# Forgetting attention in a two-layer decoder trunk: the causal mask added by VectorE, the softmax division moved to the reload of the outputs, the gate's weights in one operand

## The chip, the cores and the metric

The kernel runs on one core of a Trainium2 chip. The metric is the device time of one execution in microseconds; the time given for a kernel is the median of its runs. The core has a matrix engine (TensorE, in the profile PE, with its weight loads as PEld), a vector engine (VectorE, DVE), an engine for activation functions (ScalarE, ACT), a general engine (GpSimd, POOL) and an engine that here issues all transfers (SyncE, SP). Matrix products are accumulated in PSUM, a memory of eight banks of 128 partitions by 512 float32 numbers; everything else lies in SBUF or in DRAM.

## What is computed

A trunk of two layers on a sequence of 1024 positions with 1024 features, all in float32. Layer 0 mixes by a gated convolution, layer 1 by forgetting attention with 16 heads of 64 features; after the mixer each layer has a cross-attention into 256 memory tokens and a squared-ReLU MLP of 4096 inner features. Every sublayer is preceded by an RMS norm and added to the residual stream. The change touches the attention of layer 1:

```python
hk = rmsnorm(x, kv_norm_g)
kvf = hk @ kvf_w                       # keys, values and 16 gate columns
log_f = log_sigmoid(kvf[..., 2 * D:] + fgate_b)
c = cumsum(log_f, axis=1)              # one running sum per head
...
s = q @ k.T / sqrt(64) + (c[query] - c[key])
s = where(key_pos <= query_pos, s, -inf)
p = softmax(s)
out = (p @ v) @ w_o
```

Since `c[query]` is the same for a whole row of the softmax, it falls out; only `c[key]` has to be subtracted.

## The kernel before

The activations lie transposed: features on the partitions, in eight chunks of 128, positions along the free dimension, in two halves of 512. To keep float32 accuracy on a faster matrix format, an operand is split into a high part (a copy rounded by ScalarE) and a low part (the difference, by VectorE): `split`, lines 150 to 152. A product of two split operands is three passes (`passes`, line 262): low × high, high × low, high × high.

**The order of the work.** The program is written in the order in which the author wants it; a scheduler orders each engine's instructions ahead of the run, from that order and from its own estimate of times. Inside `in_order` blocks the order of the text is kept for the engines named. Tiles come from pools: tiles with the same `tag` share a fixed number of buffers (`bufs`), and a later tile takes a buffer that an earlier one has left. The pool `nrm` has a tag "t" with four buffers of 128 x 512, which normalization, sums of squares, loads of stored tensors and many other steps share.

**Layer 1, `fox_layer` (line 1111).** The MLP of layer 0 ends by normalizing the first half of the positions and loading the first two weight pieces (`start_fox`). `fox_layer` then prepares the gate weights `wf` as two tiles, high and low (lines 1123 to 1128), runs the first half of the first key and query products and of the gate product (24 passes, line 1136), normalizes the second half, and calls `attend`.

**`attend` (line 1155)** builds the causal mask (0 on and below the diagonal, -1e30 above), copies it and the identity matrix to the matrix format (`maskr`, `identr`), and runs two generators beside each other until the first pair of heads has keys and queries: `projections` (line 1230), which yields after every three passes, and `forget_gates` (line 1195), which forms the sigmoid's logarithm and the running sum `c` and writes it to DRAM (`cd`). Then come the 16 heads, each with eight blocks of 128 queries. For each head the row `c` is loaded back into all 128 partitions (`cj`). For each block:

- `attention_scores` (line 1294): two passes per 512 keys into one of two PSUM banks (pool `p2`), and on the last, diagonal column block a third product, identity × mask (line 1308); VectorE subtracts `cj` and takes the row maximum in one instruction (line 1310), negates it (1313); ScalarE takes the exponential and the row sum `rs` (1315); VectorE forms the reciprocal (1316) and multiplies the probabilities by it (1321; for odd blocks of the last two heads ScalarE does it, 1319).
- three blocks later (`DELAYS`), `attention_transposes` (line 1324): the probabilities are transposed by TensorE in float32 into banks of the pool `pm` (four banks) and split.
- for every second block, one step after that, `attention_output` (line 1347): 256 queries of output for one head, whose two value parts are added up by ScalarE and VectorE (`ol`), and written to DRAM (`od`, line 1359).
- three steps of the projections for the next pair of heads, as work for TensorE in between.

**The end.** Lines 1143 to 1148 load the outputs back from `od`, 16 tiles `o` of 128 x 512 (chunk by chunk, first half and second half of the positions), and split them into the operand tiles `hs`, whose buffers are free once the last projection has read the previous ones. The residual stream is loaded back from `xd` (16 transfers, line 134), and line 1153 multiplies by `fox_wo`: all eight output chunks for the first half of the positions, then all eight for the second. An output needs all eight chunks of its operand.

Of the kernel before, what the change touches and what calls it, by code (L numbers as in the profile page):

```python
# [12 lines left out]
F32 = mybir.dt.float32  # L13
F32R = mybir.dt.float32r
AF = mybir.ActivationFunctionType
ALU = mybir.AluOpType
# [70 lines left out]
def trunk(ctx, tc, a, out):  # L87
# [1023 lines left out]
    def fox_layer(xd, hs, ws, seconds):  # L1111
        nonlocal X, xpool
        cd = dram.tile([HEADS, S], F32, name="cd")
        od = dram.tile([NCH, P, S], F32, name="od")

        early = {}
        with (
            banks(4) as pm,
            tc.tile_pool(name="fs", bufs=2, space=PSUM, reuse_waits="tile") as p2,
        ):  # L1120

            with in_order({mybir.EngineType.PE, mybir.EngineType.DVE, mybir.EngineType.Activation}):
                wf = [nrm.tile([P, NCH, HEADS], F32R, name=f"wf{x}", bufs=1) for x in "hl"]
                raw = nrm.tile([P, NCH, HEADS], F32, name="wf", tag="t", bufs=4)
                nc.sync.dma_start(raw, a["wf"])
                g = par[:, COLS["kv"] : COLS["kv"] + NCH].unsqueeze(2).to_broadcast([P, NCH, HEADS])
                dve.tensor_tensor(raw, raw, g, op=ALU.mult)
                split(*wf, raw)
# [6 lines left out]
                early["gate"] = bank(pm)[:HEADS, :]  # L1135
                product(early["gate"], by_weights(wf, hs, HALVES[0]))
                normalize(hs, None, HALVES[1], rb)
                ws.append(weights(a["wv"][0], gain="kv"))
            xpool.close()
            xpool = ExitStack()  # L1140
            with tc.tile_pool(name="fa", bufs=2) as bp:
                attend(bp, p2, pm, ws, wf, hs, early, cd, od)
        hs = operands()
        for m in range(NCH):
            for sl in HALVES:
                o = nrm.tile([P, HALF], F32, name="o", tag="t", bufs=4)
                nc.sync.dma_start(o, od[m, :, sl])
# [7 lines left out]
    def attend(bp, p2, pm, ws, wf, hs, early, cd, od):  # L1155
# [12 lines left out]
        late = []  # L1168

# [11 lines left out]
        for head in range(HEADS):  # L1181
            cj = bp.tile([P, S], F32, name="cj")
            nc.sync.dma_start(cj, cd[head : head + 1, :].to_broadcast([P, S]))
            for b in range(8):
                while head not in tiles:
                    next(project)
                x = attention_scores(bp, p2, tiles[head], head, b, cj, identr, maskr)
                late.append((DELAYS[0], partial(attention_transposes, bp, pm, tiles[head], head, b, x, od)))
                late = run(late)
                for _ in range(3):  # L1190
                    next(project, None)
        while late:
            late = run(late)

    def forget_gates(bp, wf, hs, cd, early):

        fb = bp.tile([HEADS, 1], F32, name="fb", bufs=1)
# [3 lines left out]
        for sl in HALVES:  # L1201
            if sl.start == 0:
                t = early["gate"]
            else:
                t = bank(ps)[:HEADS, :]
                product(t, by_weights(wf, hs, sl))
            dve.tensor_scalar(z[:, sl], t, fb[:, 0:1], None, op0=ALU.add)
# [86 lines left out]
    def attention_scores(bp, p2, tiles, head, b, cj, identr, maskr):  # L1294
# [5 lines left out]
        mx = -3e38  # L1300
        for j in range(0, n, HALF):
# [4 lines left out]
            pe.matmul(s, qb, kh[:, sl], start=False, stop=not last)  # L1306
            if last:
                pe.matmul(s[:, b * P - j :], identr, maskr, start=False, stop=True)
# [4 lines left out]
        dve.tensor_scalar(nb, mx, -1.0, None, op0=ALU.mult)  # L1313
        rs = bp.tile([P, 1], F32, name="rs")
        act.activation(x[:, :n], x[:, :n], AF.Exp, bias=nb, accum_out=rs)  # L1315
        dve.reciprocal(rs, rs)
        if head >= HEADS - 2 and b % 2:

            act.activation(x[:, :n], x[:, :n], AF.Copy, scale=rs)
        else:  # L1320
            dve.tensor_scalar(x[:, :n], x[:, :n], rs, None, op0=ALU.mult)
# [124 lines left out]
```

## Time and profile before

| | us |
|---|---|
| median of three runs | 2823.84 |
| the three runs | 2826.63, 2823.84, 2814.29 |
| the profiled execution | 2825.31 |
| its span, first to last instruction | 2823.3 |
| TensorE busy | 2740.8 (97% of the span) |
| VectorE busy | 2030.9 (72%) |
| ScalarE busy | 1278.3 (45%) |
| start of attention to the end of its output projection, about | 1349 to 1976 |

The page of the profile gives the share of each engine over the whole span; since the stages differ, the views used below cut it by time. A row of the table by stretches begins with the bounds of the stretch in microseconds from the span's start and its length; then come the busy microseconds of PE, PEld, DVE, ACT and POOL with the number of instructions in brackets, the granted clock of TensorE (1.00 is full), the busy share of the transfer engines and what they moved in GB/s. A row of a group of instructions has the line, the engine, the operation, what is written and read, the count, the busy time, the mean in nanoseconds, and the idle time just before them with what ended it. A row in order of time has the start, the length, the engine and the line; `xN` says that N like instructions were merged. For transfers the last number is the median time from issue to landing.

### The profile page before, as it was taken

What the parts mean: (1) busy time and instruction counts of PE and PEld (TensorE: products, weight loads), DVE (VectorE), ACT (ScalarE), POOL (GpSimd) and SP (SyncE); (2) the same over time, 40 slices, a digit from 0 to 9 for tenths busy, and PEclk for the clock granted to TensorE, in tenths of its full rate; (3) what the DMA queues carried; (4) which work ended last, traced back from release to release, by engine and by line L of the source; (5) the groups of instructions that cost most, each with busy time, mean ns of one, the idle gap of its engine ahead of it and who ended that gap; (6) DMA issues with size and microseconds to landing.
All of it is one profiled execution on the core that took longest, in us unless ns stands there. A gap on an engine that the chain in (4) does not pass through costs nothing.

```text
span 2823.3 us, 36214 instructions
## 1 busy us (share of the span) xinstructions
PE 2740.8 (97%) x12968; PEld 2261.3 (80%) x12968; DVE 2030.9 (72%) x3358; ACT 1278.3 (45%) x2293; POOL 703.1 (25%) x473
## 2 busy tenths in 40 slices
PE   8999999999999999999899999989999999989998
PEld 6777777888888877888688888878888788878886
DVE  5999984555776576777788888875546855577776
ACT  5212143433555553333466666673423655543332
POOL 0000000000065625774000000000000365525773
PEclk9999999999999999999899999999999999999999
DMA  6334364322165585652222221243213455655651
GB/s 219 120 119 135 114 206 124 101 90 70 65 230 177 178 309 187 227 199 89 69 68 70 57 65 55 69 136 98 94 64 105 149 176 190 218 208 197 227 201 61
DMA packets 165428, 390.68 MB, mean 138 GB/s; under 512 B 17264, under 2 KB 46192, under 8 KB 164992
## 3 DMA queue, kind: packets, MB, share of 16 engines
q1 hardware_dynamic: 165248, 388.37, 40.9%
q8 instruction: 102, 1.67, 0.2%
q14 instruction: 78, 0.64, 0.1%
HBM read 270.79 MB, written 113.31 MB: 136 GB/s over the span
## 4 chain that ended last, share of the span: by engine, by line
PE 74%; DVE 12%; ACT 5%; DMA 5%; issue 3%; POOL 1%; SPq 0%; DVEq 0%; POOLq 0%; ACTq 0%
PE mm L1070 34%; PE mm L269 29%; PE mm L1255 5%; DVE w L148 2%; DVE op L148 2%; DVE x L408 1%; PE mm L1341 1%; DVE x L1310 1%; DMA ua<-x 1%; ACT x L1315 1%; PE mm L1353 1%; PE mm L1354 1%; DVE both L400 1%; DVE wl L148 1%; ACT pth L151 1%
## 5 line engine op out<-in xcount | busy, mean ns | idle before, releaser
L1070 PE MATMUL mm<-op,w 128*128 128x512 f32 x5424 | 1242.4, 391 | 24.5 <-ACT m L955 8.7
L1070 PEld LDWEIGHTS mm<-op,w 128*128 128x128 f32 x5424 | 1020.5, 189 | 243.2 <-ACT m L955 9.6
L269 PE MATMUL mm<-op,wh 128*128 128x512 f32 x1056 | 330.5, 394 | 4.2 <-DVE op L148 4.2
L148 DVE TENSOR_TENSOR w<-r,w 128x512 fp32r<-128x512 f32 x264 | 262.6, 998 | 30.5 <-ACT w L653 30.5
L653 ACT CAST w<-r 128x512 fp32r<-128x512 f32 x264 | 163.3, 622 | 262.0 <-PE mm L1070 233.2
L269 PEld LDWEIGHTS mm<-op,wh 128*128 128x128 f32 x1056 | 200.2, 190 | 48.5 <-DVE op L148 6.5
L1255 PE MATMUL mm<-op,wh 128*128 128x512 f32 x736 | 231.4, 396 | 0.0
L148 DVE TENSOR_TENSOR w<-t,w 128x512 fp32r<-128x512 f32 x180 | 178.2, 1005 | 63.2 <-ACT w L653 63.1
L269 PE MATMUL mm<-op,wl 128*128 128x512 f32 x528 | 210.5, 400 | 7.1 <-DVE wl L148 6.2
L207 POOL TENSOR_TENSOR r<-v,mhalf 128x4 f32<-128x4 f32 (+1 forms) x15 | 16.8, 1117 | 741.0 <-DVE v L205 741.0
L647 POOL TENSOR_TENSOR t<-r,t 128x512 f32<-128x512 f32 x104 | 174.9, 1681 | 91.4 <-DVE w L148 54.2
L653 ACT CAST w<-t 128x512 fp32r<-128x512 f32 x180 | 112.0, 622 | 169.8 <-PE mm L1070 140.6
L151 ACT CAST wh<-raw 128x1024 fp32r<-128x1024 f32 x96 | 100.7, 1050 | 193.8 <-PE mm L269 97.5
L865 POOL TENSOR_TENSOR x<-x,x 128x512 f32<-128x512 f32 x112 | 160.2, 1455 | 112.6 <-ACT x L878 101.6
L967 DVE TENSOR_TENSOR x<-mm,x 128x512 f32<-128x512 f32 x160 | 109.5, 684 | 91.1 <-PE mm L1070 73.7
L1255 PEld LDWEIGHTS mm<-op,wh 128*128 128x128 f32 x736 | 139.2, 189 | 26.7
L269 PE MATMUL mm<-op,xsh 128*128 128x512 f32 x512 | 158.0, 393 | 0.0
L1255 PE MATMUL mm<-op,wl 128*128 128x512 f32 x368 | 155.0, 421 | 1.9 <-ACT q L1275 1.9
L151 ACT CAST pth<-mm 128x512 fp32r<-128x512 f32 (+1 forms) x224 | 105.9, 495 | 108.5 <-PE mm L556 80.8
L408 DVE SCALAR_TENSOR_TENSOR x<-d,par,x 128x512 f32<-128x512 f32 x232 | 154.5, 746 | 0.0
L647 POOL TENSOR_TENSOR t<-r,r 128x512 f32<-128x512 f32 x52 | 80.2, 1542 | 295.1 <-DMA r<-in_ff_w 191.0
L1315 ACT ACTIVATE x<-x,nb 128x128 f32<-128x128 f32 (+7 forms) x128 | 99.5, 778 | 109.3 <-DVE nb L1313 100.0
(188 smaller groups left out, 4689.6 us busy)
## 6 DMA issues: line engine op xcount, KB each, us to landing
r<-in_ff_w SPq DMA_DIRECT2D x128, 512.0 KB, 4.0
op<-ua SPq DMA_DIRECT2D x80, 512.0 KB, 6.8
us<-x SPq DMA_DIRECT2D x128, 256.0 KB, 2.9
op<-us SPq DMA_DIRECT2D x64, 512.0 KB, 5.6
raw<-mvo SPq DMA_DIRECT2D x32, 512.0 KB, 3.4
ua<-ul SPq DMA_DIRECT2D x64, 256.0 KB, 2.2
ua<-uh SPq DMA_DIRECT2D x60, 256.0 KB, 2.3
raw<-in_pw SPq DMA_DIRECT2D x24, 512.0 KB, 4.7
```

The costliest lines, as they stand in the source:

```text
L148: dve.tensor_tensor(lo, src, hi.bitcast(F32), op=ALU.subtract)
L151: act.copy(hi, src)
L269: pe.matmul(out_ps, x, y, start=i == 0, stop=i == len(terms) - 1)
L400: dve.scalar_tensor_tensor(both, odd[:, j : j + n], sums[:, j : j + 1], both, op0=ALU.mult, op1=ALU.add)
L408: dve.scalar_tensor_tensor(out[s], d[:, j : j + n], w, y, op0=ALU.mult, op1=ALU.add)
L647: (dve if g in (2, 3, UP, UP + 1) else pool).tensor_tensor(t, raws[g, x], raws[g, y], op=ALU.subtract)
L653: act.copy(highs[n][0], raws[steps[n][:2]])
L865: eng.tensor_tensor(u[g, x], y1, y2, op=op_)
L967: dve.tensor_tensor(v, sums[key], v, op=ALU.add)
L1070: pe.matmul(sums[key], y, z, start=first and i == 0, stop=n == last_of[key] and i == len(terms) - 1, skip_group_check=True,)
L1255: pe.matmul(t, x, y, start=n == 0, stop=n == len(terms) - 1)
L1315: act.activation(x[:, :n], x[:, :n], AF.Exp, bias=nb, accum_out=rs)
```

## The change

In five parts:

1. **The mask.** Queries are now multiplied by -1/8, so the scores are the negative ones. The mask tile holds +1e30, stays in float32, and is added by VectorE to the diagonal column block where it lies in PSUM, instead of by a matrix product. The copies `maskr` and `identr` go.
2. **The maximum.** VectorE adds `cj` to the negative scores and takes the row minimum; the exponential gets scale -1 and the minimum itself as its bias, so the negation goes.
3. **The division.** The probabilities stay undivided. The row sums of a pair of heads are gathered in a tile of 16 columns; behind the last block of the pair (for the last pair: behind all remaining transposes and outputs) `inverse_sums` takes the reciprocals, TensorE transposes them, ScalarE copies them to a tile `ro`, and they are written to DRAM (`rd`).
4. **The reload.** With each of the 16 tiles `o` a tile `rs` of the same shape is loaded, in two transfers that each spread a row of `rd` over 64 partitions, and VectorE multiplies before the split. `rs` and `ro` have the tag "t" of the pool `nrm`, like `o`.
5. **The gate.** High and low gate weights lie in one operand of 48 columns (16 high, 16 zeros, 16 low), so that one pass gives both products: 16 passes in place of 24 for each half. ScalarE adds the bias to the low rows and VectorE adds the high rows.

```diff
@@ fox_layer
-                wf = [nrm.tile([P, NCH, HEADS], F32R, name=f"wf{x}", bufs=1) for x in "hl"]
+                wf = nrm.tile([P, NCH, 3 * HEADS], F32R, name="wf2", bufs=1)
+                dve.memset(wf.bitcast(F32), 0.0)
...
-                split(*wf, raw)
+                split(wf[:, :, :HEADS], wf[:, :, 2 * HEADS :], raw)
...
         hs = operands()
         for m in range(NCH):
             for sl in HALVES:
                 o = nrm.tile([P, HALF], F32, name="o", tag="t", bufs=4)
                 nc.sync.dma_start(o, od[m, :, sl])
+                r = nrm.tile([P, HALF], F32, name="rs", tag="t", bufs=4)
+                for i in range(2):
+                    blocks = rd[2 * m + i : 2 * m + i + 1, sl.start // P : sl.stop // P, :]
+                    nc.sync.dma_start(
+                        r[i * HD : (i + 1) * HD, :], blocks.rearrange("h b q -> h (b q)").to_broadcast([HD, HALF])
+                    )
+                dve.tensor_tensor(o, o, r, op=ALU.mult)
                 split(*(x[:, sl] for x in hs[m]), o)
@@ new
+    def gate_product(t, wf, hs, sl):
+        for k in range(NCH):
+            for i, x in enumerate(hs[k]):
+                pe.matmul(t[: 3 * HEADS, :], wf[:, k, :], x[:, sl], start=k + i == 0, stop=k + i == NCH)
@@ attend
-        mask = nrm.tile([P, P], F32, name="mask", tag="t", bufs=4)
-        make_causal_mask(nc, mask, mask_val=-1e30)
-        maskr, identr = (bp.tile([P, P], F32R, name=n, bufs=1) for n in ("maskr", "identr"))
-        dve.tensor_copy(maskr, mask)
-        dve.tensor_copy(identr, ident)
+        mask = bp.tile([P, P], F32, name="mask", bufs=1)
+        make_causal_mask(nc, mask, mask_val=1e30)
...
+        def inverse_sums(pair, rs):
+            dve.reciprocal(rs, rs)
+            t = bank(pm)[:16, :P]
+            pe.transpose(t, rs, ident)
+            o = nrm.tile([P, HALF], F32, name="ro", tag="t", bufs=4)[:16, :P]
+            act.copy(o, t)
+            nc.sync.dma_start(rd[2 * pair : 2 * pair + 2, :, :].rearrange("h b q -> (h b) q"), o)
...
+            if head % 2 == 0:
+                rs = bp.tile([P, 16], F32, name="rs")
...
+            if head % 2 and head + 1 < HEADS:
+                inverse_sums(head // 2, rs)
         while late:
             late = run(late)
+        inverse_sums(HEADS // 2 - 1, rs)
@@ forget_gates
-            dve.tensor_scalar(z[:, sl], t, fb[:, 0:1], None, op0=ALU.add)
+            act.activation(z[:, sl], t[2 * HEADS : 3 * HEADS, :], AF.Identity, bias=fb[:, 0:1])
+            dve.tensor_tensor(z[:, sl], t[:HEADS, :], z[:, sl], op=ALU.add)
@@ put_queries
-        act.activation(q, t, AF.Copy, scale=1.0 / math.sqrt(HD))
+        act.activation(q, t, AF.Copy, scale=-1.0 / math.sqrt(HD))
@@ attention_scores
             if last:
-                pe.matmul(s[:, b * P - j :], identr, maskr, start=False, stop=True)
-            m = bp.tile([P, 1], F32, name=f"mx{j}")
-            dve.tensor_tensor_reduce(x[:, sl], s, cj[:, sl], 1.0, mx, ALU.subtract, ALU.max, m)
-            mx = m
-        nb = bp.tile([P, 1], F32, name="nb")
-        dve.tensor_scalar(nb, mx, -1.0, None, op0=ALU.mult)
-        rs = bp.tile([P, 1], F32, name="rs")
-        act.activation(x[:, :n], x[:, :n], AF.Exp, bias=nb, accum_out=rs)
-        dve.reciprocal(rs, rs)
-        if head >= HEADS - 2 and b % 2:
-            act.activation(x[:, :n], x[:, :n], AF.Copy, scale=rs)
-        else:
-            dve.tensor_scalar(x[:, :n], x[:, :n], rs, None, op0=ALU.mult)
+                dve.tensor_tensor(s[:, b * P - j :], s[:, b * P - j :], mask, op=ALU.add)
+            m = bp.tile([P, 1], F32, name=f"mn{j}", bufs=4)
+            dve.tensor_tensor_reduce(x[:, sl], s, cj[:, sl], 1.0, mn, ALU.add, ALU.min, m)
+            mn = m
+        act.activation(x[:, :n], x[:, :n], AF.Exp, bias=mn, scale=-1.0, accum_out=rs)
```

More of the change, by code (lines that the diff above doesn't have):

```diff
@@ L1114, in fox_layer @@
         od = dram.tile([NCH, P, S], F32, name="od")
+        rd = dram.tile([HEADS, 8, P], F32, name="rd")
         early = {}
@@ L1134, in fox_layer @@
                 rb = spread(r)
-                early["gate"] = bank(pm)[:HEADS, :]
-                product(early["gate"], by_weights(wf, hs, HALVES[0]))
+                early["gate"] = bank(pm)
+                gate_product(early["gate"], wf, hs, HALVES[0])
                 normalize(hs, None, HALVES[1], rb)
@@ L1186, in attend @@
                     next(project)
-                x = attention_scores(bp, p2, tiles[head], head, b, cj, identr, maskr)
+                k = head % 2 * 8 + b
+                x = attention_scores(bp, p2, tiles[head], b, cj, mask, rs[:, k : k + 1])
                 late.append((DELAYS[0], partial(attention_transposes, bp, pm, tiles[head], head, b, x, od)))
@@ L1204, in forget_gates @@
             else:
[L1205 to L1207 removed]
+                t = bank(ps)
+                gate_product(t, wf, hs, sl)
+            act.activation(z[:, sl], t[2 * HEADS : 3 * HEADS, :], AF.Identity, bias=fb[:, 0:1])
+            dve.tensor_tensor(z[:, sl], t[:HEADS, :], z[:, sl], op=ALU.add)
         yield
@@ L1292, in put_values, with attention_scores @@
         return transposed
-    def attention_scores(bp, p2, tiles, head, b, cj, identr, maskr):
+    def attention_scores(bp, p2, tiles, b, cj, mask, rs):
         kh, kl, qs, _, _ = tiles
```

10 lines of the change are left out of this document (5 added, 5 removed).

## The prediction, as it was put down before the changed kernel was run

> **What bounds the kernel now.** I read the page first, then the table by stretches, then the queue that issues the transfers, then single engines in order of time. The page's first line gives the length of the traced execution; its own time was 2825.31 us, so 2.0 us lie outside the span, and it stands 1.5 us above the median of the three runs (2823.84, with one run at 2814.29).
>
> ```profile
> span 2823.3 us, 36214 instructions
> ```
>
> The table by stretches has, after the bounds and the length, the busy time of PE, PEld, DVE, ACT and POOL, then PE's granted clock.
>
> ```profile
> 1649.70:1711.80 62.10, 61.67 (x370) 53.72 (x369) 52.48 (x147) 38.11 (x83) 2.01 (x2) 1.00 0.22 60
> ...
> 1840.00:1888.00 48.00, 38.93 (x256) 32.25 (x255) 43.49 (x129) 40.77 (x88) 0.00 (x0) 1.00 0.28 85
> 1888.00:1976.00 88.00, 88.00 (x393) 72.77 (x392) 43.78 (x56) 29.50 (x40) 1.01 (x1) 1.00 0.43 140
> ```
>
> Three regimes are to be seen. One pair of heads in the middle takes 62.10 us and TensorE is busy 61.67 of them: there every TensorE instruction counts, and VectorE has 9.6 us to spare. In the last 48 us of attention TensorE idles 9 us, while VectorE (43.49) and ScalarE (40.77) are nearly full: this tail is bound by their chain. Then the output projection runs, TensorE full for 88 us. So each edit is priced by the regime in which it lies.
>
> The next view is the queue that issues transfers, in order of time: the reload of the attention outputs (`o<-od`) and, behind it, of the residual stream.
>
> ```profile
> 1462.91 0.32 SPq L1147 DMA_DIRECT2D o<-od  x1
> ...
> 1841.64 6.72 SPq L1147 DMA_DIRECT2D o<-od  x7
> ...
> 1889.33 0.33 SPq L1147 DMA_DIRECT2D o<-od  x1
> 1889.69 9.70 SPq L134 DMA_DIRECT2D x<-xd  x16
> ```
>
> Of the 16 reloads, the first is issued at 1462.91, as soon as pair 0 is written, and seven go out in a row from 1841.64 while attention still runs; only the last waits for attention's end. That overlap is what I expect to go.
>
> **The reload.** Its tiles `o` have the tag "t" with four buffers. The change allocates from the same tag a second tile `rs` per reload and, inside attention, one tile `ro` per pair, the last of them in `inverse_sums` behind the whole head loop. What decides is in which order tiles of one tag are handed out. The first layer of this trace answers that.
>
> ```profile
> L218 DVE SCALAR_TENSOR_TENSOR h<-x,par,mm x16: 741/744/750, 24.5 to 59.4; 128x512 f32<-128x512 f32 x16
> ...
> 425.20 0.62 ACT L182 ACTIVATE t<-x 128x512 f32<-128x512 f32 x1
> ...
> 425.39 0.34 SPq L323 DMA_DIRECT2D x<-in_xT  x1
> ```
>
> Line 323 loads a kernel input, which is there from the start, into a tile of tag "t"; the last `h` of that layer, another tile of the tag, was written at 59.4 us. Yet the first such load is issued at 425.39 us, 0.19 us behind the start of the instruction that writes the last sum-of-squares tile `t`, its predecessor in the text. Tiles of a tag are thus handed out strictly in the order of the program. In the changed kernel the first `o` stands behind the last `ro`, so no reload can be issued before the last pair's sums are copied to `ro`. All 16 reloads leave the tail and follow attention.
>
> When is that? The last exponential and the end of attention, as ScalarE, TensorE and the chain that ended last show them:
>
> ```profile
> 1879.42 1.16 ACT L1315 ACTIVATE x<-x,nb 128x1024 f32<-128x1024 f32 x1
> ```
>
> ```profile
> 1886.17 0.28 PE L1354 MATMUL mm<-pth,vs 128*128 128x128 f32 x1
> ```
>
> ```profile
> 1887.36 47.03 PE mm L269 x206
> ```
>
> The transposition of the sums takes its PSUM bank behind the last output product, so it follows 1886.4; with ScalarE's copy the reload opens at about 1887 (in times of the kernel before).
>
> Four buffers hold two reloads with their `rs`. One round of a buffer pair:
>
> ```profile
> cj<-cd SPq DMA_DIRECT2D x16, 512.0 KB, 4.2
> od<-ol SPq DMA_DIRECT2D x64, 64.0 KB, 1.9
> o<-od SPq DMA_DIRECT2D x16, 256.0 KB, 2.8
> x<-xd SPq DMA_DIRECT2D x16, 256.0 KB, 5.6
> ```
>
> ```profile
> L148 DVE TENSOR_TENSOR op<-o,op 128x512 fp32r<-128x512 f32 x15 | 10.2, 683 | 1.4 <-ACT op L151 1.4
> ...
> L1321 DVE TENSOR_SCALAR x<-x,rs 128x640 f32<-128x640 f32 (+3 forms) x6 | 3.1, 524 | 0.0
> L1316 DVE RECIPROCAL rs<-rs 128x1 f32<-128x1 f32 x13 | 2.1, 160 | 1.0 <-ACT x L1315 0.8
> L1313 DVE TENSOR_SCALAR nb<-mx 128x1 f32<-128x1 f32 x13 | 1.8, 142 | 0.0
> ```
>
> ```profile
> L151 ACT CAST op<-o 128x512 fp32r<-128x512 f32 x15 | 8.8, 629 | 2.0 <-DMA o<-od 2.0
> L1319 ACT ACTIVATE x<-x,rs 128x512 f32<-128x512 f32 (+3 forms) x7 | 6.1, 878 | 0.2 <-DVE rs L1316 0.2
> ```
>
> Issue of `o` and of one `rs` half 0.65 (two of 0.32); landing of the last 2.8 (a broadcast of 128 KB, between the 64 KB write of 1.9 and the 512 KB broadcast of 4.2; I take the 256 KB load); multiplication 0.68 and low part 0.68 on VectorE; high part 0.63 on ScalarE; four handoffs, which I put at 0.1 each. That is 5.9 us for two reloads. TensorE needs the eighth chunk's first half, the 15th reload, before it can finish even the first output: eight rounds, 47 us, so 1934. It may meanwhile do the first seven chunks of two outputs (weights have two buffers), 42 of the projection's 384 products; 342 remain, at 47.03/206 = 0.228 us about 78.1 us, ending at 2012. Before, it ended at 1887.4 + 384 × 0.228, 1975. **Reload: +37** (rounds of 5.2 to 6.5 us: +32 to +42).
>
> The Trainium skill, page "Trainium Kernel Development and Optimization", section Best Practices, asks for two buffers to overlap transfers with compute; by it the reload would cost only VectorE's time, which is the third rival below. Here two reloads in flight don't cover a landing: per round 3.5 us of transfer stand against 2 us of compute.
>
> The 16 loads of the residual stream are set free at the same moment; before they were issued over 9.7 us and landed 5.6 us behind their issue, and their 4 MB share the queue with the first rounds. They may cost nothing, or all of these 15 us; two or three rounds whose landing takes 5.6 in place of 2.8 are the nearest, **+6** (0 to +15).
>
> During the rounds TensorE works sparsely, and its clock falls. The stretches after the idle time at the start of this layer:
>
> ```profile
> 1361.00:1365.00 4.00, 3.87 (x14) 3.38 (x14) 2.49 (x5) 0.43 (x2) 0.00 (x0) 0.51 0.32 123
> 1365.00:1368.00 3.00, 3.00 (x8) 2.40 (x9) 0.16 (x1) 0.00 (x0) 1.01 (x1) 0.52 0.00 0
> ```
>
> Seven microseconds ran at 0.51 and 0.52 of the clock. The same at the projection's dense start costs half of that, **+3** (0 to +4).
>
> **The masks.** Each block's mask product (line 1308) goes from TensorE to VectorE.
>
> ```profile
> 1654.85 0.22 PE L1308 MATMUL mm<-maskr,identr 128*128 128x128 f32 x1
> 1654.91 0.27 PE L1341 MATMUL mm<-ident,x 128*128 128x128 f32 x1
> ...
> 1673.68 0.27 PE L1308 MATMUL mm<-maskr,identr 128*128 128x128 f32 x1
> 1673.79 0.33 PE L1353 MATMUL mm<-ptl,vs 128*128 128x256 f32 x1
> ```
>
> It holds TensorE until the next start: 0.06 us in most blocks, 0.11 where the product before it is as short (the last column block is 128 wide in 4 of 16). Mean 0.07, 16 per pair, 1.1 us; over the seven TensorE-bound pairs **-8** (-6 to -10). VectorE's add of 128 columns in PSUM is not in this trace; the nearest row is a 128x128 subtraction from PSUM:
>
> ```profile
> 1655.72 0.29 DVE L148 TENSOR_TENSOR ptl<-mm,pth 128x128 fp32r<-128x128 f32 x1
> ```
>
> At 0.2 to 0.35 us, 16 per pair are 3 to 6 us, while 16 negations (0.142), 16 reciprocals (0.160) and about as many normalizations (0.524) leave, 13 us: VectorE has more room than before, and its spare 9.6 us hide the add. Without that cover it would cost up to 4.6 us per pair. The Trainium skill, page "VectorE: DVE Perf Modes", section on the TRN2 errata, speaks against it: every instruction pays a fixed cost, so operations should have 512 elements or more. By its figures for PSUM the add is an estimated 0.26 us; the row agrees, and the sum stays.
>
> New is a wait at each pair's end: TensorE's transposition of the sums follows the block's own exponential with no block of slack, where other transposes have three (`DELAYS`). Behind it in the same bank order stand the transposes of older blocks; values' projection can fill in. Nothing, or 1.5 us at each of seven ends: **+2** (0 to +10).
>
> **The gate.** Its 48 products become 32:
>
> ```profile
> L269 PE MATMUL mm<-op,wfh 128*16 128x512 f32 x32 | 10.0, 394 | 0.0
> L269 PE MATMUL mm<-op,wfl 128*16 128x512 f32 x16 | 6.4, 399 | 0.0
> ```
>
> 16 × 0.228 = 3.7 us of TensorE; the evacuation gains a ScalarE instruction of about 0.6 us, beside which the projections of pair 0 run. **-3** (0 to -4).
>
> **The tail.** Without the reloads VectorE loses 10.2 us and ScalarE 8.8; besides, 3.1 + 2.1 + 1.8 and 6.1 us of normalizing go, and 13 masks come (3 to 5 us). Both fall below TensorE's 38.93 of 48, whose 9 idle us shrink, but the chain of the last blocks stays: **-5** (-1 to -8).
>
> **Sum:** 37 + 6 + 3 - 8 + 2 - 3 - 5 = +32, on 2825.3: **2857 us**. All low ends give +10, all high ends +64.
>
> **Rivals.** (1) The reload isn't held: `o` and `rs` are fetched beside the tail as before, because the order of tiles that line 323 shows has another cause. For it speaks that 15 of 16 reloads are split before 1888 now. Then the tail carries 15 more multiplications (9 us) and 3 to 5 us of masks for 7 us less on VectorE, so about +2 in place of -5, 37, 6 and 3: 2825 - 8 + 2 - 3 + 2 = 2818, not slower. It decides for this side wherever the first reload is issued before the last exponential. (2) The pair ends stall: TensorE waits out a block's scores, reduction and exponential, about 4.5 us, seven times: +31 in place of +2, 2886. Against it: other work can fill in. (3) The rounds overlap fully: only VectorE's two passes of 0.68 count, 15 × 1.36 = 20 us in place of 47: 2830. Against it: two reloads in flight. Should TensorE gain nothing from the masks, the forecast is 2865.
>
> **Chances.** Forecast 0.75; rivals 0.13, 0.08 and 0.04. A measurement of this kernel tells 0.5%, 14 us, from no change. Faster 0.05 (the lower part of rival 1), within 0.5% 0.13 (the rest of 1, rival 3), slower 0.82. The range 2832 to 2884 leaves out rivals 1 and 3 and most of 2; it holds the forecast's bounds less their joint extremes.
>
> **What would show it.** The first `o<-od` behind the last exponential, and TensorE mostly idle for some 40 us ahead of the output projection; if an `o` is issued near 1460, the main step is wrong. A middle pair at about 61 us confirms the masks; TensorE waits at the transposed sums would show rival 2. If TensorE isn't starved behind attention, I am wrong by 40 us.

## The result, and the profile after

The changed kernel takes 2852.89 us, median of 4 runs (2848.83 to 2860.57); the kernel before, on the same chip, 2822.45 us (2814.29 to 2826.63). The ratio is 1.0115, with a 95% interval of 1.0080 to 1.0149. The prediction was 2857 (2832 to 2884).

The profiled execution took 2856.77 us in all. From the page, its span:

```profile
span 2855.0 us, 35812 instructions
```

Five instants that both traces show cut the span into stages: the layer's first product; the load of the fourth head's row of cumulated gates (`cj<-cd`); that of the sixteenth head's; the end of the last product of attention; and the start of the second dense block of the output projection in the chain that ended last. The rows of the dense products are, for the second block of the kernel before, and for both blocks of the changed kernel:

```profile
1935.32 40.50 PE mm L269 x178
```

```profile
1933.39 38.70 PE mm L269 x158
...
1973.02 40.49 PE mm L269 x178
```

| stage (us) | before | after | difference | predicted |
|---|---|---|---|---|
| start to the layer's first product | 1349.56 | 1354.01 | +4.45 | 0 |
| to the load of head 4's row | 105.16 | 104.43 | -0.7 | -4 |
| six pairs, to the load of head 16's row | 372.56 | 367.72 | -4.8 | -5 |
| tail, to the end of attention | 59.17 | 52.40 | -6.8 | -5 |
| reload, to the second dense block | 48.87 | 94.46 | **+45.6** | +46 |
| rest of the kernel | 887.98 | 881.98 | -6.0 | 0 |

The first and last rows are code that no edit touches. They wander: in the 13 traces of this study the first lies between 1344.4 and 1354.5 us, the last between 881.1 and 888.0. No part of the change explains these movements, so stages are a better measure than totals for anything under some 5 us.

So the whole loss stands behind attention. The queue that issues transfers, in order of time (start, duration, queue, line, transfer, count), in the changed kernel:

```profile
1876.10 0.58 SPq L1150 DMA_DIRECT2D o<-od  x1
1879.43 0.45 SPq L1382 DMA_DIRECT2D od<-ol  x1
1879.97 0.53 SPq L1191 DMA_DIRECT2D rd<-ro  x1
1880.56 1.10 SPq L1154 DMA_DIRECT2D rs<-rd  x2
1881.71 0.58 SPq L1150 DMA_DIRECT2D o<-od  x1
1882.39 1.08 SPq L1154 DMA_DIRECT2D rs<-rd  x2
1883.57 0.53 SPq L134 DMA_DIRECT2D x<-xd  x1
...
1924.30 0.33 SPq L1150 DMA_DIRECT2D o<-od  x1
1925.67 1.09 SPq L1154 DMA_DIRECT2D rs<-rd  x2
1926.81 4.55 SPq L134 DMA_DIRECT2D x<-xd  x9
```

No reload goes out before 1876.10, where the kernel before issued its first at 1462.91. Between the first and the last lie 48 us, in which two `o` and their broadcasts are in flight at a time, with one load of the residual stream slipped into each round. One round, from the chain that ended last:

```profile
1889.34 3.21 DMA rs<-rd
...
1892.67 0.70 DVE o L1157
...
1893.39 0.63 ACT op L151
...
1894.05 0.70 DVE op L148
...
1894.77 0.44 SPq L1154
...
1895.26 3.54 DMA rs<-rd
```

From one broadcast to the next it is 5.92 us: 3.21 of landing, 2.03 of computing in a row on two engines (multiplication, high part, low part), 0.44 of issue, the rest handoffs. TensorE meanwhile, in order of time (the bracket is the idle time ahead and what ended it), and the same stretch by windows (bounds and length; busy time of PE, PEld, DVE, ACT, POOL; granted clock; DMA share, GB/s):

```profile
1886.04 0.80 PE L269 MATMUL mm<-op,wl 128*128 128x512 f32 x1 [7.37 <-ACT op L151]
...
1927.81 1.22 PE L269 MATMUL mm<-op,wl 128*128 128x512 f32 x2 [3.40 <-ACT op L151]
...
1933.39 0.79 PE L269 MATMUL mm<-op,wl 128*128 128x512 f32 x1 [2.66 <-DVE wl L148]
```

```profile
1878.56:1886.02 7.46, 0.10 (x1) 0.00 (x0) 1.11 (x3) 1.24 (x3) 0.00 (x0) 0.66 0.49 147
1886.02:1927.79 41.77, 21.45 (x42) 12.35 (x42) 19.38 (x29) 8.64 (x14) 0.00 (x0) 0.54 0.66 212
1927.79:1933.39 5.60, 2.93 (x6) 1.77 (x6) 4.64 (x7) 3.47 (x6) 0.00 (x0) 0.50 0.92 301
1933.39:1937.00 3.61, 3.61 (x9) 2.83 (x10) 2.89 (x4) 1.12 (x3) 0.00 (x0) 0.50 1.05 387
1937.00:1939.00 2.00, 2.00 (x6) 1.61 (x5) 0.00 (x0) 0.00 (x0) 0.00 (x0) 0.51 0.58 227
1939.00:1973.00 34.00, 34.00 (x155) 28.08 (x155) 18.72 (x24) 12.55 (x18) 0.00 (x0) 1.00 0.26 82
```

7.5 us pass before the first operand, 41.8 in seven rounds (5.97 each) in which 42 products are done, and 5.6 more with six products and a wait for weights. At the dense rate of the kernel before (0.228 us) and with its 0.91 us of start, these 48 products are 11.9 us; 54.8 were taken, so 43 are lost. Then the first 5.6 us of the dense block run at half the clock: its 158 products take 38.70 us, where at the dense rate they are 36.1, so 2.6 more are lost. That is the 45.6.

### The profile page after: what moved, and what is told of

It reads as the page before. It is cut to its first block, busy times and chain, and to the rows that moved or that the text cites. A ratio compares the mean times of both kernels' runs of the same rounds, so it can differ in the third digit from the quotient of the medians.

```text
span 2855.0 us, 35812 instructions
## 1 busy us (share of the span) xinstructions
PE 2745.2 (96%) x12832; PEld 2259.6 (79%) x12832; DVE 2001.2 (70%) x3133; ACT 1277.1 (45%) x2295; POOL 697.8 (24%) x473
## 4 chain that ended last, share of the span: by engine, by line
PE 76%; DVE 12%; DMA 5%; ACT 3%; issue 3%; SPq 0%; POOL 0%; DVEq 0%; POOLq 0%; ACTq 0%
PE mm L1070 34%; PE mm L269 27%; PE mm L1286 7%; DVE x L408 2%; DVE op L148 2%; DVE w L148 2%; PE mm L1364 2%; PE mm L1377 1%; DVE both L400 1%; PE mm L1376 1%; PE mm L1336 1%; PE mm L1337 1%; DMA rs<-rd 1%; DVE wl L148 1%; DVE x L967 1%
## 5 line engine op out<-in xcount | busy, mean ns | idle before, releaser
L1070 PE MATMUL mm<-op,w 128*128 128x512 f32 x5424 | 1242.5, 391 | 21.4 <-DVE x L967 7.1
L269 PE MATMUL mm<-op,wh 128*128 128x512 f32 x1056 | 338.5, 404 | 4.4 <-DVE op L148 4.2
L269 PE MATMUL mm<-op,wl 128*128 128x512 f32 x528 | 215.6, 411 | 36.1 <-ACT op L151 27.5
L1286 PE MATMUL mm<-op,wh 128*128 128x512 f32 x736 | 231.7, 396 | 0.0
L967 DVE TENSOR_TENSOR x<-mm,x 128x512 f32<-128x512 f32 x160 | 109.5, 684 | 92.5 <-PE mm L1070 72.3
L1286 PE MATMUL mm<-op,wl 128*128 128x512 f32 x368 | 156.2, 424 | 1.8 <-ACT q L1306 1.8
L269 PEld LDWEIGHTS mm<-op,wl 128*128 128x128 f32 x528 | 102.2, 195 | 66.9 <-ACT op L151 33.2
```

The costliest lines, as they stand in the source:

```text
L269: pe.matmul(out_ps, x, y, start=i == 0, stop=i == len(terms) - 1)
L967: dve.tensor_tensor(v, sums[key], v, op=ALU.add)
L1070: pe.matmul(sums[key], y, z, start=first and i == 0, stop=n == last_of[key] and i == len(terms) - 1, skip_group_check=True,)
L1286: pe.matmul(t, x, y, start=n == 0, stop=n == len(terms) - 1)
```

## The experiments

The square of hold and division comes first, then the other parts, then how the hold works. The stage times of all runs stand in a table behind them.

**e1: the last small tile out of the tag.** The tile that carries the inverse sums comes from the tag of the output tiles.

```diff
-            o = nrm.tile([P, HALF], F32, name="ro", tag="t", bufs=4)[:16, :P]
+            o = bp.tile([HD, 2 * P], F32, name="ol")[:16, :P]
```

> The changed kernel with one edit: the small tile that carries a pair's inverse sums out comes from the tag of the output tiles (ol) and no longer from tag t, in which the reloads stand. Theory (the last such tile, standing ahead of the reloads in the order of the program, holds all 16 reloads behind attention): the reloads go out during attention again, as soon as pair 0 is written; the 7 rounds of 5.97 us between attention and the output projection go but for the last, about 40 us less than the changed kernel: 2815 us (2806 to 2825), at or below the kernel before. Rival A (the division at the reload, with its broadcasts and multiplications, costs the time wherever it stands): within 10 us of the changed kernel, 2843 to 2860. Rival B (the queue of transfers holds them, not the tag): first reload still behind the last exponential, 2853.

Measured 2833.86 us, ratio to the kernel before 1.0032 (1.0017 to 1.0047): between theory and rival A. Rival B falls, since the reloads are free again, in SP's order of time:

```profile
1463.86 0.32 SPq L1150 DMA_DIRECT2D o<-od  x1
1464.27 1.11 SPq L1154 DMA_DIRECT2D rs<-rd  x2
1478.02 0.33 SPq L1150 DMA_DIRECT2D o<-od  x1
...
1837.74 1.10 SPq L1154 DMA_DIRECT2D rs<-rd  x2
1838.94 0.54 SPq L1150 DMA_DIRECT2D o<-od  x1
...
1895.56 0.33 SPq L1150 DMA_DIRECT2D o<-od  x1
```

They start at 1463.86, but the last is issued at 1895.56, 17 us behind the end of attention. Windows show why they didn't get through in the tail:

```profile
1837.00:1878.19 41.19, 35.94 (x236) 29.46 (x234) 38.62 (x107) 30.83 (x72) 0.00 (x0) 1.00 0.31 90
```

VectorE is busy 38.62 of 41.19 us there, and got to six of the 16 multiplications, after three before it. Seven follow attention, in the same slow rounds. Without the hold the reload costs 72.3 us in place of 94.5, not 49.

**e3: the hold alone,** in the kernel before.

```diff
         while late:
             late = run(late)
+        t = bank(pm)[:16, :P]
+        pe.transpose(t, x[:, :16], ident)
+        o = nrm.tile([P, HALF], F32, name="ro", tag="t", bufs=4)[:16, :P]
+        act.copy(o, t)
+        nc.sync.dma_start(rd[HEADS - 2 : HEADS, :, :].rearrange("h b q -> (h b) q"), o)
```

> The kernel before with one addition: behind the head loop a 16x128 tile of tag t is written (a transposition of the last block, a copy, a transfer), ahead of the reloads in the order of the program. No division moves, no mask moves, no broadcast is loaded. Theory (the order of the tag alone holds the reloads): all 16 reloads follow attention. Four buffers are in flight: a buffer comes round in about 4.9 us (issue 0.33, landing 2.8, high part 0.63, low part 0.68, handoffs), four rounds, so the 15th reload is ready some 21 us behind attention in place of 42; TensorE can do 42 of the 384 products (9.6 us) meanwhile; the tail gains up to 5: +6 to +14 us on the kernel before, 2829 to 2837. Rival A (division is the cost): as the kernel before, 2818 to 2826, with reloads in the tail. Rival B (the hold is the whole cost, however many buffers): +30 or more, 2852.

Measured 2839.53 us, 1.0048 (1.0033 to 1.0063). In SP's order of time:

```profile
1887.32 1.22 SPq L1148 DMA_DIRECT2D o<-od  x1
1891.14 0.53 SPq L1199 DMA_DIRECT2D rd<-ro  x1
1891.77 0.85 SPq L1148 DMA_DIRECT2D o<-od  x2
...
1909.61 0.32 SPq L1148 DMA_DIRECT2D o<-od  x1
```

One small tile, used by nothing, moves all 16 reloads behind 1887. With four in flight they take 22 us. The stage grows by 16.5 us, the tail shrinks by 1.8. By the medians the size is 2.5 us above the theory's upper bound, by the ratio (+13.6 us) just inside it; TensorE's wait for the third output's weights, 3.15 us here, is the part that the theory hadn't counted.

**e6: the hold without the division.** The changed kernel without `rs`; outputs aren't divided.

```diff
-                r = nrm.tile([P, HALF], F32, name="rs", tag="t", bufs=4)
...
-                dve.tensor_tensor(o, o, r, op=ALU.mult)
```

> The changed kernel without the tiles rs at the reload: no broadcasts of the inverse sums and no multiplications, so its outputs aren't divided by the sums; the tile of inverse sums in tag t stays ahead of the reloads. Theory (hold times rounds): the reloads still follow attention, now four in flight and not two; the 15th is ready some 21 us behind attention in place of 42, so 15 to 25 us less than the changed kernel: 2828 to 2838. Rival A (the division is all of the cost): as the kernel before or under it, 2810 to 2822. Rival B (the hold is all, rounds don't matter): 2848 to 2857.

Measured 2825.16 us, 1.0012 (0.9996 to 1.0028), below the theory and above rival A. The stage explains it: 63.8 us, 15 over the kernel before. The theory's working had taken 15 to 25 off the stage of the changed kernel; 30.6 went.

**e10: neither.** The edits of e1 and e6 together; outputs aren't divided.

> The changed kernel with both edits at once: the tile of inverse sums comes from the tag of the output tiles, and the reload has no tiles rs, no broadcasts and no multiplications (outputs aren't divided by the sums). It is the fourth corner of a square: from attention's last product to the second, dense block of the output projection the kernel before takes 48.9 us, the changed kernel 94.5, with the hold alone taken away 72.3, with the division alone taken away 63.8. Theory (the loss is the hold and the depth of the reload, and nothing else of the change): 48 to 51 us with neither, a tail of 52 to 55, the whole 8 to 14 us below the kernel before, 2809 to 2815. Rival (something else of the change costs too: the sums' transpositions and their transfers, or the masks in the tail): over 56 us there, 2818 or more.

Measured 2811.76 us, 0.9971 (0.9959 to 0.9983); the stage is 49.6 us, as before the change, and the rival falls. The square, in us from attention's end to the dense block: neither 49.6, hold alone 63.8 (+14), division alone 72.3 (+23), both 94.5 (+45). The two are 8 us dearer together than added.

**e11: two in flight without the division.** Meant to separate the number in flight from the broadcasts and multiplications; outputs aren't divided.

```diff
                 r = nrm.tile([P, HALF], F32, name="rs", tag="t", bufs=4)
-                for i in range(2):
...
-                dve.tensor_tensor(o, o, r, op=ALU.mult)
+                pool.memset(r[:, :1], 0.0)
```

> The changed kernel with the tiles rs still allocated at the reload from tag t, but with nothing in them except one column that GpSimd sets: no broadcasts and no multiplications (outputs aren't divided by the sums). So the reloads are held as before and two are in flight, as in the changed kernel, where the run without the tiles has four. Depth theory: a round is the reload alone (issue 0.33, landing 2.8, high part 0.63, low part 0.68, handoffs 0.4), 4.9 us in place of 5.97; from attention's end to the dense block 85 to 88 us (changed kernel 94.5, four in flight 63.8): 2842 to 2848. Rival (the broadcasts and multiplications themselves are the cost, not the depth): 62 to 67 us there, 2823 to 2828.

Measured 2824.53 us, 1.0018 (1.0002 to 1.0034), and 64.1 us in the stage: the rival's number, but the run doesn't bear it out. The setting of one column takes 0.10 us, so a tile `rs` gives its buffer back at once and the next reload takes it. The 16 reloads go out within 22.1 us (1868.19 to 1890.32), as in e6 within 21.4. It is the same experiment as e6, and how the 30.6 us divide between the smaller number in flight and the longer round stays open. An estimate from the rows: a round without broadcasts and multiplications would still hold the landing of an `o` (3.2), high and low part (0.63 and 0.70) and the issue (0.33), 4.9 us, and seven such rounds are some 8 us shorter than seven of 5.97. By that most of the 30.6 would belong to the number in flight, but no run shows it.

**e4: the masks alone,** in the kernel before: VectorE's mask, queries by -1/8, minima; normalization and gate as before.

```diff
-                pe.matmul(s[:, b * P - j :], identr, maskr, start=False, stop=True)
+                dve.tensor_tensor(s[:, b * P - j :], s[:, b * P - j :], mask, op=ALU.add)
...
-        nb = bp.tile([P, 1], F32, name="nb")
-        dve.tensor_scalar(nb, mx, -1.0, None, op0=ALU.mult)
```

> The kernel before with the mask and minimum part alone: queries scaled by -1/8, the mask added in PSUM by VectorE, minima in place of negated maxima; reciprocal and normalization stay in attention, the gate as before. Theory (TensorE sets the pairs): a middle pair 61.0 to 61.4 us in place of 62.1, seven of them; in the last 48 us of attention, where VectorE is nearly full, 13 additions of 0.29 us come and 13 negations of 0.14 go, +2: 2815 to 2820, 3 to 8 us less than the kernel before. Rival (the addition stands in the path of each block's scores, TensorE waits for the bank): no gain or a loss, 2822 to 2832.

Measured 2816.23 us beside 2823.16 for the kernel before, 0.9976 (0.9963 to 0.9989): the time and the middle pair are as the theory has them, while the tail, for which it gave +2, is 1.7 us shorter. One middle pair, by windows:

```profile
1641.78:1703.14 61.36, 60.33 (x354) 52.36 (x353) 54.24 (x147) 38.03 (x83) 2.14 (x2) 1.00 0.21 61
```

61.36 us in place of 62.10, though VectorE now carries masks and normalization both (54.24 of 61.36). TensorE's busy time fell by 1.34 us (61.67 to 60.33), of which 0.6 came back as idle time. By its ratio this is the best of the kernels that leave nothing out, 0.24% below the kernel before and so better than both; the intervals of e5, e8 and e9 overlap with its own.

**e5 and e7: the gate,** added to e4 (e5) and taken out of the changed kernel (e7, whose edit is shown).

```diff
-                wf = nrm.tile([P, NCH, 3 * HEADS], F32R, name="wf2", bufs=1)
...
-            act.activation(z[:, sl], t[2 * HEADS : 3 * HEADS, :], AF.Identity, bias=fb[:, 0:1])
-            dve.tensor_tensor(z[:, sl], t[:HEADS, :], z[:, sl], op=ALU.add)
+            dve.tensor_scalar(z[:, sl], t, fb[:, 0:1], None, op0=ALU.add)
```

> The run with the mask part alone (2816.2) plus the gate part: one operand of 48 columns, 32 products in place of 48, the two evacuations. Normalization stays in attention. From the layer's first product to the fourth load of a row of sums the kernel before takes 105.2 us, the mask part alone 107.2, the changed kernel 104.4. Theory A (16 products fewer are worth their 2 to 4 us of TensorE there, although the chain to the first cumulated sum is longer): 104 to 105 us for that stretch, 2812 to 2815. Theory B (the longer chain costs what the products save): 107 us or more, 2815 to 2819.

> The changed kernel with the gate as it was: high and low weights in two operands, 48 products, one evacuation on VectorE. Without normalization in attention four kernels with the new gate took 104.4 to 105.2 us from the layer's first product to the fourth load of a row of sums. Theory A (16 products fewer gain): 106.5 to 107.5 us there, 2 to 3 us above the changed kernel. Theory B (the gate is worth nothing; which instructions are put where at the start decides): 104 to 106 us, within 2 us of the changed kernel.

e5: 2815.82 us, 0.9987 (0.9977 to 0.9997); e7: 2846.93 us, 1.0102 (1.0068 to 1.0135). To the fourth row e5 takes 105.6 us, 1.6 less than e4 without the new gate; e7 takes 103.6, 0.8 less than the changed kernel with it. In the next pair of runs the new gate costs 1.6. So e5's stretch lies between the two theories' ranges and e7's below both. The sign changes from pair to pair, which fits theory B in that no effect above some 2 us shows either way; four kernels in which the text of this stretch is the same (after, e6, e11, e12) differ by as much, 104.3 to 106.1. One thing is steady in all three pairs: with the new gate the first load of a row of cumulated gates comes 0.8 to 1.9 us later behind the layer's first product (55.0 to 56.4 us with the old gate, 55.9 to 57.3 with the new one).

**e8 and e9: the division for the last pair only,** on e4 and on e5.

```diff
+                if m == NCH - 1:
+                    r = nrm.tile([P, HALF], F32, name="rs", tag="t", bufs=4)
...
+                    dve.tensor_tensor(o, o, r, op=ALU.mult)
...
+        if head >= HEADS - 2:
+            k = (head - HEADS + 2) * 8 + b
+            act.activation(x[:, :n], x[:, :n], AF.Exp, bias=mn, scale=-1.0, accum_out=sums[:, k : k + 1])
+            return x
```

> The run with the mask part alone (2816.2), and the division at the reload for the last pair of heads only: pairs 0 to 6 are normalized in attention as before and reloaded beside it, four in flight; only the two reloads of the eighth chunk carry a broadcast and a multiplication, and the tile of inverse sums comes from the tag of the output tiles. Theory (normalizing costs time only in the tail, where VectorE and ScalarE are full, and one round of two reloads hides behind the 42 products of the first seven chunks, 9.6 us): tail 52 to 54 us in place of 57.5, then 49 to 53 us in place of 49.7 to the dense block: 2811 to 2816. Rival (TensorE waits for the eighth chunk: write, broadcast, multiplication and split take longer than the products that can go first): 57 us or more there, 2817 to 2824.

> The same with the gate part as well. By theory A of the gate 2 to 3 us below the run without it (2808 to 2814), by theory B the same or 1 to 2 above.

e8: 2817.02 us, 0.9988 (0.9976 to 1.0001); e9: 2816.67 us, 0.9987 (0.9973 to 1.0001). By the ratio neither gains on the kernel without it (e4 0.9976, e5 0.9987), and e8's tail and time are 1 us above the theory's ranges. The tail gave 2.5 us (55.0 in place of 57.5), and the reload took 3.3 back (53.0 in place of 49.7). In e8's TensorE, the waits behind attention:

```profile
1890.32 0.50 PE L269 MATMUL mm<-op,wl 128*128 128x512 f32 x1 [1.56 <-DVE wl L148]
...
1903.45 0.50 PE L269 MATMUL mm<-op,wl 128*128 128x512 f32 x1 [1.92 <-DVE wl L148]
```

These waits are for weights, not for the eighth chunk: the first two outputs end close together, so both weight buffers come free late, and the third output's weights are then split on a VectorE that has a reload to do; the second wait comes two outputs later.

**e12: the reloads on GpSimd's queue.** In the changed kernel the first `o` is issued at 1876.10, ahead of the copy that the prediction said it waits for. From ScalarE's order of time:

```profile
1878.98 0.25 ACT L1190 COPY ro<-mm 16x128 f32<-16x128 f32 x1
```

```diff
-                nc.sync.dma_start(o, od[m, :, sl])
+                nc.gpsimd.dma_start(o, od[m, :, sl])
...
-                    nc.sync.dma_start(
+                    nc.gpsimd.dma_start(
```

> The changed kernel with the 16 reloads and their 32 broadcasts issued from GpSimd's queue and not from SP's; tags, multiplications and splits as they are. The question is how the tag holds the reload: in the changed kernel the first one is issued 2.9 us before the last pair's sums are copied out, so it doesn't wait for that copy. Queue theory (the tag's order decides only where the reloads stand in the queues, there behind the stores of the attention outputs): on GpSimd's queue, idle since 1786, the first reloads go out long before attention's end, 1790 to 1860; the multiplications still stand behind the last minimum on VectorE, so little comes of it, 84 to 92 us from attention's end to the dense block in place of 94.5, 2842 to 2851. Buffer theory (the first reload's buffer is free only when an earlier tile of the tag has been read): first reload at 1876 or later, 94 to 98 us there, 2851 to 2858.

Measured 2856.17 us, 1.0128 (1.0101 to 1.0155), within the buffer theory's range, but 100.5 us in the stage, more than either theory gave. GpSimd's order of time, then the last two stores of `ro` on SP:

```profile
1787.57 0.73 POOL L1150 DMA_DIRECT2D o<-od  x1
1788.30 1.04 POOL L1154 DMA_DIRECT2D rs<-rd  x2
1824.64 0.57 POOL L1150 DMA_DIRECT2D o<-od  x1 [35.29 <-ACT pth L151]
1873.45 1.04 POOL L1154 DMA_DIRECT2D rs<-rd  x2 [48.24 <-ACT op L151]
```

```profile
1822.61 0.33 SPq L1191 DMA_DIRECT2D rd<-ro  x1
...
1871.59 0.33 SPq L1191 DMA_DIRECT2D rd<-ro  x1
```

Both theories hold a part. The first `o` and its broadcasts find free buffers and go out at 1787, so the changed kernel's first reload was kept back by its place in SP's queue, behind all but the last of the stores of the attention outputs. The second `o` goes out 2.0 us behind the store of pair 6's `ro`, the second `rs` 1.9 us behind that of the last pair's. That fits the tag's four buffers: each pair's `ro` has one of them until it is stored, and a later tile must wait for it (the events that the brackets name have another line and tile, so they are not taken as the cause here). And even the reload that landed early was multiplied only at 1871.66: on VectorE its instructions stand behind those of attention. Then the 16 loads of the residual stream were issued in a row from 1872.55 on SP; the broadcasts issued before 1880 landed in 5.8 us at the median, the later ones in 3.1.

The stages of all runs (us; "row" is the load of a row of cumulated gates; the ratio is to the kernel before):

| run | ratio | to row 4 | rows 4 to 16 | tail | to dense block |
|---|---|---|---|---|---|
| before | 1 | 105.2 | 372.6 | 59.2 | 48.9 |
| after | 1.0115 | 104.4 | 367.7 | 52.4 | 94.5 |
| e1 no hold | 1.0032 | 104.8 | 367.7 | 54.9 | 72.3 |
| e6 no division | 1.0012 | 104.6 | 367.7 | 52.4 | 63.8 |
| e10 neither | 0.9971 | 105.2 | 367.7 | 55.3 | 49.6 |
| e11 empty `rs` | 1.0018 | 106.1 | 367.7 | 52.4 | 64.1 |
| e12 GpSimd's queue | 1.0128 | 104.3 | 367.7 | 52.4 | 100.5 |
| e7 old gate | 1.0102 | 103.6 | 368.0 | 52.4 | 92.6 |
| e3 hold in before | 1.0048 | 106.1 | 372.6 | 57.4 | 65.3 |
| e4 masks | 0.9976 | 107.2 | 368.2 | 57.5 | 49.7 |
| e5 masks, gate | 0.9987 | 105.6 | 368.4 | 57.5 | 49.2 |
| e8 last pair | 0.9988 | 104.5 | 369.4 | 55.0 | 53.0 |
| e9 last pair, gate | 0.9987 | 106.2 | 369.3 | 55.1 | 54.7 |

## Why the prediction was right, and where it was not

The time, the sign and the place were right; the sizes of the smaller terms were not all.

- **Reload, +37: right in mechanism and size, 38.7.** Held by the tag (e1 and e3 show it from both sides), rounds of 5.97 us (5.9 predicted), the 15th reload's low part started 49.2 us behind attention's end (47 predicted). In these 49.2 us 42 products are done, which with the start are 10.5 at the dense rate. The landing of a broadcast was taken at 2.8 us and measured at 3.2 in the middle; the handoffs came out smaller.
- **One sentence of that step was too strict**: "no reload can be issued before the last pair's sums are copied". The first `o` was issued 2.9 us before that copy, and e12 shows that one whole reload can go out some 80 us earlier. The order of the tag set the place in the queues of SP and VectorE, and held one buffer of four. It cost the forecast nothing, since the first broadcast and the second reload stood behind the copy anyway.
- **Contention of the residual stream, +6: not there.** The step took the 16 loads as set free at the same moment; in SP's queue they stood one to a round, and the rounds were within 0.1 us of the forecast made without them. A broadcast landed in 3.2 us at the median, in e1 beside attention, with none of these loads under way, in 3.0. In e12, where all 16 did go out among the first rounds, the stage is 6.0 us longer than in the changed kernel, though that run differs in the queue as well.
- **Weights, not in the sum: +2.7.** The third output's weights had to wait for buffers that two interleaved outputs gave back late. Together with 1.7 more for the reload and 1.2 more for the clock it makes up for the contention that didn't come, so the stage's +45.6 meets +46 in part by chance.
- **Clock, +3: 4.2.** The rounds ran at 0.54 of the clock at no cost, as TensorE waited anyway. But the last six products ahead of the dense block, at 0.50, took 2.9 us in place of 1.4, and the dense block then spent 5.6 us at 0.50 and 0.51 before it had the full clock, which cost 2.6. The length isn't fixed: these 158 products took 37.5 to 38.7 us in the six kernels that keep the hold (after, e3, e6, e7, e11, e12). The Trainium skill, page "TensorE: Matmul & The Clock Gate", section "Part 1: The HAM clock gate", gives about 3.4 us of sustained work at half the clock; here the rows measure 5.6, and the measurement stands.
- **Masks, -8, and pair ends, +2: right in their sum, each smaller.** Six pairs gave 4.8 us, 0.81 each; the forecast, -8 and +2 over seven, was 0.86 each. But the masks alone (e4) gave 4.4 over six pairs, 0.73 each in place of 1.1, which over seven is 5 and below the term's range of 6 to 10: more of TensorE's time was saved than the step had counted, and part of it came back as waits. The mask's addition is 294 ns in the middle (0.2 to 0.35 predicted; the row gives shortest, middle and longest).

```profile
L1339 DVE TENSOR_TENSOR mm<-mm,mask x128: 279/294/300, 1409.9 to 1870.2; 128x128 f32<-128x128 f32 x128
```

  Where TensorE waited for VectorE at the score banks and at the pair ends (us in total, times, longest):

```profile
PE mm L1336 <- DVE mn L1342: 5.7, 11, 1.1
PE mm L1188 <- DVE rs L1186: 1.3, 7, 0.2
```

  0.2 us per pair end: rival 2 falls. The addition takes 0.294 us for 128 columns, the low part of an operand 0.683 for 512, so a quarter of the width takes well over a quarter of the time; VectorE had room for it. By the Trainium skill, page "VectorE: DVE Perf Modes", section on the TRN2 errata, the addition was an estimated 0.26 us, and its rule that small operations pay a fixed cost agrees.
- **Gate, -3: failed.** "16 × 0.228 = 3.7 us of TensorE" are saved, but TensorE isn't the bound there: from 1390 to 1416.8 the chain that ended last runs through VectorE, ScalarE and transfers alone. The step's second half, an extra instruction "beside which the projections of pair 0 run", lies in the chain to the first score. The rows below are the evacuations, first of the kernel before, then of the changed kernel; they begin 34.7 and 35.0 us behind the layer's first product, but in the changed kernel VectorE's additions follow, and they end at 37.2 in place of 36.1. e5, e7 and e9 show an effect of either sign, under 2 us.

```profile
1384.25 1.39 DVE L1207 TENSOR_SCALAR x<-mm,fb 16x512 f32<-16x512 f32 x2
```

```profile
1389.03 1.25 ACT L1237 ACTIVATE x<-mm,fb 16x512 f32<-16x512 f32 x2
```

```profile
1389.95 1.27 DVE L1238 TENSOR_TENSOR x<-mm,x 16x512 f32<-16x512 f32 x2
```

- **Tail, -5: -6.8.** Masks in place of negations gained 1.7 (e4). The other 5.1 (57.5 to 52.4) are two things: without normalizing, but with the reloads still beside it, the tail is 55.3 (e10), 2.2 less; the reloads' leaving gives the remaining 2.9.

- **Rivals.** (1) falls: the first reload is issued at 1876.10, behind the last exponential (1872.12 to 1873.3), and e1 gives what it would have been, though at 2834 and not 2818, since a released reload doesn't get through the full tail. (3) falls as well: rounds of 5.97 us are not 1.36 a reload. Two reloads were in flight, and still 3.2 us of landing stood open in every round. The Trainium skill, page "Trainium Kernel Development and Optimization", section Best Practices, asks for two buffers to overlap transfers with compute; here two weren't enough.

That the profiled run came out at 2856.77 against 2857 is luck in part: the untouched stages added -1.5 between them, and the median is 2852.89.

## What to carry to other kernels

Before a tile is added to a shared tag, look at what stands behind its last use in the order of the program: here it was the prefetch on which the whole next stage leans, and one 16x128 tile put all of it behind attention. Work taken off an engine that has room to spare (VectorE's normalization in the pairs) gains next to nothing there (0.5 us over six pairs, e4 against the changed kernel) and is paid in full where it lands, here in a stage with one round of transfers in flight at a time. And read a part's worth in the stage where it lies: the masks were worth their 0.7 to 0.8 us per pair all along, under a loss of 45 elsewhere.

## What the runs showed of the hardware

- Two outputs that advance together release their weights together: in seven kernels in which the first two outputs advance together (after, e1, e3, e6, e7, e11, e12) TensorE waited 2.7 to 3.4 us for the third output's weights, in the kernel before not at all.
- The place in a queue holds a transfer as firmly as a buffer does: the first reload was issued 522 us behind the layer's first product from SP's queue (1876.10) and 441 us behind it from GpSimd's (1787.57, in e12).
- Stages that no edit touches moved by up to 10 us from trace to trace (the first of the table above), so a gain of 2 us is to be read from its stage and not from the total.
